# A hybrid layer on one core: three sets of RWKV scores, the inverse inside the neighbour's chain, and output-projection pools laid out anew

## The chip, the cores and the metric

The kernel runs on one core of a Trainium2 chip. The metric is device time in microseconds (us) of one launch; the median of three runs is 2404.65 us (2397.96 to 2404.76).

## The reference, cut to what matters

```python
xn = rms_norm(h, norm1_gain); proj = xn @ w_in            # 2048 x 1024 @ 1024 x 3840
ret = silu(gate) * head_norm(retention(q, k, v))          # 4 heads of 128, chunks of 64
rw = rwkv7_time_mix(...)                                  # 8 heads of 64, a strict recurrence
...
def step(state, inp):                                     # RWKV-7, per token
    sa = einsum('bhvk,bhk->bhv', state, a_t)
    state = state * w_t + sa * b_t + v_t * k_t
    return state, einsum('bhvk,bhk->bhv', state, r_t)
...
h = h + concatenate([ret, rw]) @ w_out
h = h + hier_moe(rms_norm(h, norm2_gain), ...)            # best of 4 groups, best 2 of its 8 experts
return rms_norm(h, final_norm_gain)
```

All 2048 tokens are one sequence; data are float32.

## The kernel before, in words

The program is written as a stream of operations with priorities; a scheduler that knows each tile's readers and writers turns the stream into one fixed queue for each engine (PE for matmuls, DVE, ACT and POOL for elementwise work, SP for issuing transfers). An engine runs its queue strictly in order, so an instruction that waits holds back all that stands behind it. A tile is a buffer out of a pool: a pool of n buffers lets n tiles live at once, the next waits until the oldest has no readers left. Pools are opened from the left or the right end of the on-chip memory, and what is opened later on the same end may lie over a pool that was closed, and then waits for its last users.

**Phase A, about 0 to 1260 us.** Four groups g of 512 tokens. `norm_b` scales eight slices of x into `nT`; `rwkv_proj` and `ret_head` project them with W_in. Each float32 product is three matmuls over a high and a low part of both factors (`split_w` makes the parts on ACT and DVE). Retention then runs `core(g, h)` for four heads, each a chain of matmuls in the PSUM pool `pk` of one bank with evictions between them; the very last head, (3, 3), takes the pool `pj` of two banks instead. The projection matmuls `pj<-nT,whl` are long and independent, and fill PE wherever something else waits.

RWKV runs in 16 units u of 128 tokens, in steps:

- `rwkv_prep(u)`: loads features, forms decays, makes the score tiles `ar` and `pt` (matmuls `pb<-ar,bk`), and `bkt`, `uv`, `bon`, `wc` for the chain;
- the solve (labelled solve{u} in the stream, inside `rwkv_prep`): pieces of `pt` go to DRAM (`nl_d`) and come back as `ln`, POOL runs 62 small instructions `tm`, `xl` one after the other, and SP stores `xl_d` and loads it back as `t1s`, `t2s` and `inv`;
- `rwkv_inv(u)`: a transpose of `t1s` on PE, called the turn here (`psi<-cst,t1s`), and eight small matmuls with evictions complete the inverse;
- `rwkv_chain(u)`: two halves c that carry the state `sbd`: `psr`, times the inverse into `psz`, `uv`, `pss_`, output `yt`;
- `rwkv_fin(u)`: head norm of `yt`, gate, and the store `mx_d<-yt`.

In the group loop the calls stand in the order prep(u), inv(u), fin(u-2), chain(u-1), and the last fin and chain follow behind the loop.

**Phase B, about 1260 to 1560 us.** `tile2(t)` is W_out on 16 token tiles: eight k-slices of the mixed rows `mx_d` come back, are split into `mT`, and 48 matmuls `acc<-wo,mT` fill two PSUM banks of the pool `accr` (three banks). DVE adds the residual rows (`w<-in_x_dram` for tiles 0 to 7 from the pool `hxp` of three buffers, `raw<-in_x_dram` for 8 to 15 from the pool `rwp` of eight). `post(tiles)`, for one or two tiles, stores h, transposes it with the constant `ct`, computes router logits with `wrt`, runs some 45 small DVE operations for the top choices, scales the rows with `g2b` into `xt_d`, and sums the choices (`os`) on PE for the slot numbers. The constants ct, g2b, wrt, brt, g2c lie in the pool `k2`, the small router tiles in `s2`, both on the right end.

**Phase C, 1560 us to the end.** The experts: weights arrive by DMA, PE is busy without a break. Nothing in it moves but names of buffers.

Of the kernel before, what the change touches and what calls it, by code (L numbers as in the profile page):

```python
# [34 lines left out]
NFS = 6  # L35
FB = (2, 2, 2, 2, 2, 2, 2, 1, 1)
# [96 lines left out]
def build(tc, A, out, dbg=None, phases=3):  # L133
# [17 lines left out]
    def mm(o, l, r, start=True, stop=True):  # L151
        PE.matmul(o, l, r, start=start, stop=stop)  # L152
# [31 lines left out]
    gc, xp, ntp = gp("gc", 1), gp("xp", 1), gp("ntp", 1)  # L184
    wh, wr, ev, rk, rc = gp("wh", 3), gp("wr", 4), gp("ev", 3), gp("rk", 2), gp("rc", 4)
    pj, pkb = gp("pj", 2, space=PSUM), gp("pk", 1, space=PSUM)
    if True:
# [93 lines left out]

        def norm_a(g):
# [14 lines left out]
            xs = []  # L297
            for k in range(8):
                xs.append(xp.tile([128, 512], F32, name=f"x{k}"))
                SY.dma_start(xs[k], A["xt"][k * 128:(k + 1) * 128, g * G:(g + 1) * G])  # L300
# [5 lines left out]
        def norm_b(g):  # L306
# [7 lines left out]
            for k in range(8):  # L314
                n = ntp.tile([128, 2, 512], F32R, name=f"nT{k}")
                with soon():
                    (GP if k in XPL else V).tensor_tensor(xs[k], xs[k], rsb, op=ALU.mult)
                    SC.activation(n[:, 0], xs[k], AF.Copy, scale=g1c[:, k:k + 1])
                    V.scalar_tensor_tensor(n[:, 1], xs[k], g1c[:, k:k + 1], n[:, 0].bitcast(F32),  # L319
                                           op0=ALU.mult, op1=ALU.subtract)  # L320
                nT.append(n)
            return nT

        def lora(g, fo):
# [7 lines left out]
            def job(j, f):  # L332
# [5 lines left out]
                t = xp.tile([128, 512], F32, name=f"x{j * 4 + f}")  # L338
# [44 lines left out]
        def rwkv_prep(u):  # L383
            t0 = u * 128
            mk(f'prep{u}')
            ar = rp.tile([128, 4, 2, 128], F32, name="ar", bufs=2)
            pt = rp.tile([128, 4, 2, 2, 128], F32, name="pt", bufs=2)
            bkt = rp.tile([128, 2, 512], F32, name="bkt", bufs=2)
            uv = rp.tile([128, 2, 512], F32, name="uv", bufs=2)
            bon = rp.tile([128, 4, 128], F32, name="bon", bufs=3)  # L390
            wc = rp.tile([128, 4, 2], F32, name="wc", bufs=2)
# [5 lines left out]
            c8 = lambda x: x.rearrange("p (c t) -> p c t", t=64)  # L397
            lg = tr.tile([128, 128], F32, name="lg", bufs=3)
            kt, sg_, ta, rt, vt = tmp(), tmp(), tmp(), tmp(), tmp()
# [42 lines left out]
            psb = pb.tile([128, 4, 128], F32, name="pb")  # L442
            mm(psb.rearrange("p f t -> p (f t)"), blk2, rt)
            V.tensor_tensor(bon, psb, f3(vt), op=ALU.mult)
            psv = pb.tile([128, 512], F32, name="pb")
            for i in range(4):
                PE.transpose(psv[:, i * 128:(i + 1) * 128], f3(vt)[:, i], ident)
            uvh = uv.rearrange("p c (f h v) -> p c f h v", h=2, v=64)
            GP.memset(uvh[0:64, :, :, 0], 0.0)
            GP.memset(uvh[64:128, :, :, 1], 0.0)  # L450
            for c in range(2):
                pv = psv[c * 64:c * 64 + 64].rearrange("p (f h v) -> p f h v", h=2, v=64)
                SC.copy(uvh[64:128, c, :, 0], pv[:, :, 0])
                SC.copy(uvh[0:64, c, :, 1], pv[:, :, 1])
            for i in range(0, 4, 2):
# [10 lines left out]
                pst = pb.tile([128, 2, 2, 128], F32, name="pb")  # L466
                for q in range(4):
                    PE.transpose(pst[:, q % 2, q // 2], bk[:, i * 2 + q], ident)
                SC.copy(bkt[:, :, i * 128:(i + 2) * 128], pst.rearrange("p c f x -> p c (f x)"))
# [19 lines left out]
            for q in range(4):  # L489
                SY.dma_start(xl_d[u].rearrange("l (r q) t -> q l r t", q=4)[q], xl[q * 32:(q + 1) * 32])  # L490
            ST[u] = (ar, pt, bkt, uv, bon, wc, lg)

        def rwkv_inv(u):
# [17 lines left out]
            PE.transpose(ps[:, 0].rearrange("p f x -> p (f x)"), t1s.rearrange("p f x -> p (f x)"), ident)  # L511
# [12 lines left out]
        def rwkv_chain(u):  # L524
            ar, pt, bkt, uv, bon, wc, lg = ST.pop(u)
            tt = inv_[u % 2]
            mk(f'chain{u}')
            for c in range(2):
# [19 lines left out]
                for f in range(4):  # L548
                    mm(pss_[:, f], bkt[:, c, f * 128:(f + 1) * 128], uv[:, c, f * 128:(f + 1) * 128], f == 0, f == 3)
# [105 lines left out]
        for g in range(NG):  # L655
# [7 lines left out]
            for u in range(u0, u0 + 4):  # L663
                with tc.high_priority(offset=PRW):
                    rwkv_prep(u)
                with tc.high_priority(offset=PRC):
                    rwkv_inv(u)
                if u >= 2:
                    with tc.high_priority(offset=PRF):
                        rwkv_fin(u - 2)  # L670
                if u >= 1:
                    with tc.high_priority(offset=PRC):
                        rwkv_chain(u - 1)
            if g == NG - 1:
                with tc.high_priority(offset=PRC):
                    rwkv_fin(4 * NG - 2)
                    rwkv_chain(4 * NG - 1)
                    rwkv_fin(4 * NG - 1)
# [14 lines left out]
    rwp, tpp, accl = lp("rwp", NRAW), lp("tpp", 2, space=PSUM), lp("accl", 3, space=PSUM)  # L693
# [647 lines left out]
```

## Time and profile before

| what | value |
|---|---|
| median of 3 runs | 2404.65 us |
| the profiled execution's own time | 2402.56 us |
| its span on the core | 2400.8 us |
| mean granted TensorE clock | 0.954 of full speed |
| PE busy, DVE busy, ACT busy | 2196.5, 1698.5, 1157.2 us |
| first matmul of the output projection | 1260.2 us |
| first matmul of the experts' phase | 1560.1 us |

The profiled execution is 2.1 us under the median. PE is the engine to watch: what matters is where it stands idle and what ended that idle time, and the clock at which it ran.

### The profile page before, as it was taken

How to read it: one execution, taken by the hardware profiler on the slowest of the kernel's cores; microseconds unless marked ns; L12 is line 12 of the kernel's file. 1: busy time of each engine (PE TensorE's matmuls, PEld its weight loads, DVE VectorE, ACT ScalarE, POOL GpSimd, SP SyncE). 2: the span in 40 equal slices, each digit the busy share in tenths (PEclk: the TensorE clock that was granted, in tenths of full speed). 3: DMA queues.
4: the chain of work that ended last, by engine and by line, in shares of the span. 5: the costliest groups of instructions: out<-in, count | busy, mean ns of one | idle time of the engine just before them, and what ended most of it. 6: DMA issues, size and time to landing. Idle time of an engine off the chain costs nothing. (4 is left out here: it accounts for less than half of the span.)

```text
span 2400.8 us, 36373 instructions
## 1 busy us (share of the span) xinstructions
PE 2196.5 (91%) x11816; PEld 1803.3 (75%) x11817; DVE 1698.5 (71%) x3594; ACT 1157.2 (48%) x1963; POOL 779.1 (32%) x1405
## 2 busy tenths in 40 slices
PE   5999889998998989999879999599999999999990
PEld 4887678887777877788768888577777777777770
DVE  4477775878766787667775665767777777777775
ACT  4353443434434344343332232267777677776763
POOL 2036444354531575146541433411112111111110
PEclk9999899999999999999969999799999999999995
DMA  6643254433544325433234445289999999999978
GB/s 212 211 148 99 82 172 135 135 94 99 173 142 122 98 88 167 125 101 99 84 96 130 127 163 175 94 304 306 307 321 299 304 300 320 310 293 303 310 233 297
DMA packets 291298, 454.78 MB, mean 189 GB/s; under 512 B 93392, under 2 KB 164496, under 8 KB 291088
## 3 DMA queue, kind: packets, MB, share of 16 engines
q1 hardware_dynamic: 277136, 414.10, 51.7%
q0 software_dynamic: 13824, 37.80, 7.0%
q8 instruction: 94, 1.54, 0.3%
q14 instruction: 100, 0.82, 0.1%
q10 hardware_dynamic: 144, 0.52, 0.1%
HBM read 375.18 MB, written 81.85 MB: 190 GB/s over the span
## 5 line engine op out<-in xcount | busy, mean ns | idle before, releaser
L152 PE MATMUL pj<-nT,whl 128*128 128x512 f32 x2496 | 628.1, 403 | 9.2 <-DVE nT L319 5.2
L152 PEld LDWEIGHTS pj<-nT,whl 128*128 128x128 f32 x2496 | 466.3, 192 | 107.0 <-DVE nT L319 5.7
L914 DVE TENSOR_TENSOR hl<-raw,hl 128x1024 fp32r<-128x1024 f32 x384 | 448.5, 1219 | 121.5 <-ACT hl L913 121.5
L152 PE MATMUL acc<-hl,xT 128*128 128x512 f32 (+1 forms) x2048 | 508.1, 400 | 0.0
L152 PEld LDWEIGHTS acc<-hl,xT 128*128 128x128 f32 (+1 forms) x2048 | 365.0, 182 | 100.0 <-ACT xT L172 0.2
L913 ACT CAST hl<-raw 128x1024 fp32r<-128x1024 f32 x384 | 378.4, 1048 | 6.7 <-PE tp L152 3.0
L249 ACT CAST whl<-wraw 128x512 fp32r<-128x512 f32 x248 | 152.5, 618 | 299.3 <-PE pj L152 236.1
L250 DVE TENSOR_TENSOR whl<-wraw,whl 128x512 fp32r<-128x512 f32 x248 | 188.0, 761 | 144.2 <-ACT whl L249 138.1
L152 PE MATMUL acc<-hl,hT 128*128 128x512 f32 (+1 forms) x1024 | 249.5, 398 | 0.0
L152 PEld LDWEIGHTS acc<-hl,hT 128*128 128x128 f32 (+1 forms) x1024 | 183.1, 181 | 51.8
L486 POOL TENSOR_TENSOR tm<-xl,ln 128x60 f32<-128x60 f32 (+24 forms) x496 | 173.8, 350 | 105.2 <-DMA ln<-nl_d 60.4
L488 POOL TENSOR_TENSOR xl<-xl,tm 128x60 f32<-128x60 f32 (+24 forms) x496 | 195.3, 394 | 36.6
L152 PE MATMUL acc<-wo,mT 128*128 128x512 f32 x768 | 192.3, 402 | 0.0
L1147 POOL DMA_INDIRECT h_d<-yo,ti x48 | 80.1, 1670 | 299.3 <-ACT yo L1139 180.1
L1014 POOL DMA_INDIRECT xb<-xt_d,ti x48 | 49.5, 1031 | 369.6 <-PE tp L1025 288.0
L152 PEld LDWEIGHTS acc<-wo,mT 128*128 128x128 f32 x768 | 142.3, 191 | 28.7 <-DVE mT L169 0.2
L152 PE MATMUL pj<-whl,nT 128*128 128x256 f32 x768 | 114.3, 298 | 0.3 <-DVE gs L600 0.2
L464 DVE TENSOR_TENSOR pt<-pb,cst 64x512 f32<-64x512 f32 x128 | 88.0, 687 | 22.6 <-PE pb L152 20.8
L152 PEld LDWEIGHTS pj<-whl,nT 128*128 128x128 f32 x768 | 101.6, 199 | 3.0 <-DVE gs L600 0.5
L499 POOL COPY mbd<-pt 32x128 f32<-32x128 f32 x64 | 20.7, 323 | 222.9 <-DVE pt L464 199.1
L172 ACT CAST xT<-tp 128x512 fp32r<-128x512 f32 x80 | 47.0, 588 | 82.6 <-PE tp L1025 54.4
L152 PE MATMUL pb<-ar,bk 64*128 64x128 f32 x512 | 76.3, 295 | 5.2 <-DVE pt L464 3.7
(445 smaller groups left out, 3184.5 us busy)
## 6 DMA issues: line engine op xcount, KB each, us to landing
raw<-in_wg_dram SPq DMA_DIRECT2D x128, 512.0 KB
raw<-in_wu_dram SPq DMA_DIRECT2D x128, 512.0 KB
raw<-in_wd_dram SPq DMA_DIRECT2D x128, 512.0 KB
wraw<-in_win_dram SPq DMA_DIRECT2D x208, 256.0 KB
tr<-pf_d SPq DMA_DIRECT2D x80, 256.0 KB
pf_d<-ev SPq DMA_DIRECT2D x52, 256.0 KB
x<-in_xt_dram SPq DMA_DIRECT2D x32, 256.0 KB
pf_d<-x SPq DMA_DIRECT2D x32, 256.0 KB
```

The costliest lines, as they stand in the source:

```text
L152: PE.matmul(o, l, r, start=start, stop=stop)
L172: SC.copy(dst_h, ps)
L249: SC.copy(hl[:, 0], raw)
L250: V.tensor_tensor(hl[:, 1], raw, hl[:, 0].bitcast(F32), op=ALU.subtract)
L464: V.tensor_tensor(pt[zs, i:i + 2, :, z ^ h], psp[h][zs].rearrange("p (f c) x -> p f c x", f=2), maskp[zs, None, None, :].to_broadcast([64, ...
L486: GP.tensor_tensor(tv, xl[:, 0:r, t:t + 1].to_broadcast([128, r, n]), ln[:, t:t + 1, t + 1:32].to_broadcast([128, r, n]), op=ALU.mult)
L488: GP.tensor_tensor(xl[:, 0:r, t + 1:32], xl[:, 0:r, t + 1:32], tv, op=ALU.add)
L499: GP.tensor_copy(mbd[i * 32:(i + 1) * 32, :, i * 32:(i + 1) * 32], pt[i % 2 * 64:i % 2 * 64 + 32, :, i // 2, 0, 32:64])
L913: (SC.copy if hi is SC else hi.tensor_copy)(hl[:, 0], raw)
L914: lo.tensor_tensor(hl[:, 1], raw, hl[:, 0].bitcast(F32), op=ALU.subtract)
L1014: return GP.indirect_dma_start(out=xbs[b], out_offset=None, in_=xt_d, in_offset=bass.IndirectOffsetOnAxis(ap=ti[b][:, e:e + 1], axis=0), b ...
L1147: GP.indirect_dma_start(out=h_d, out_offset=bass.IndirectOffsetOnAxis(ap=idx, axis=0), in_=y, in_offset=None, bounds_check=S + 127, comput ...
```

## The change

Instruction counts by engine are the same before and after; only order, waits and memory places differ. There are four parts.

1. The tiles `ar`, `pt`, `wc` get three buffers instead of two, and in `rwkv_prep` the part that makes `bon`, `uv`, `bkt` stands behind the solve instead of ahead of it.
2. `rwkv_inv(u + 1)` is called inside `rwkv_chain(u)`, behind the `pss_` matmuls of the first half, and a dependency that costs no semaphore keeps the turn behind them. The loop runs prep(u), chain(u-2), fin(u-3).
3. The ring of x slices has four tiles instead of eight, `wr` three instead of four buffers, and head (3, 3) of retention uses `pk` like the others.
4. The pool `accr` becomes `accs` (one bank) and `accr` (two), taken in turn; each weight tile `wo` has a pool of its own; loading pools `mrp` and `mxp` are larger and apart; splits of the weights and of the first three tiles have the chain's priority; `k2`, `s2` and `rwp` lie on the left end now, over RWKV's pools.

```diff
-            ar = rp.tile([128, 4, 2, 128], F32, name="ar", bufs=2)
-            pt = rp.tile([128, 4, 2, 2, 128], F32, name="pt", bufs=2)
+            ar = rp.tile([128, 4, 2, 128], F32, name="ar", bufs=3)
+            pt = rp.tile([128, 4, 2, 2, 128], F32, name="pt", bufs=3)
...
-        def rwkv_inv(u):
+        def rwkv_inv(u, behind):
...
-            PE.transpose(ps[:, 0].rearrange("p f x -> p (f x)"), t1s.rearrange("p f x -> p (f x)"), ident)
+            turned = PE.transpose(ps[:, 0].rearrange("p f x -> p (f x)"), t1s.rearrange("p f x -> p (f x)"), ident)
+            if behind:
+                tc.add_manual_dep(turned.ins, behind.ins.name, mybir.DependencyInfo(
+                    mybir.DependencyClass.NoSync, mybir.DependencyReason.DATA))
...
-                    mm(pss_[:, f], bkt[:, c, f * 128:(f + 1) * 128], uv[:, c, f * 128:(f + 1) * 128], f == 0, f == 3)
+                    last = mm(pss_[:, f], bkt[:, c, f * 128:(f + 1) * 128], uv[:, c, f * 128:(f + 1) * 128], f == 0, f == 3)
+                if c == 0 and u + 1 < 4 * NG:
+                    rwkv_inv(u + 1, last)
...
-            pk = pj if (g, h) == (NG - 1, 3) else pkb
-            pkn = "pj" if pk is pj else "pk"
+            pk, pkn = pkb, "pk"
...
+            for u in range(u0, u0 + (4 if g < NG - 1 else 7)):
+                if u < 4 * NG:
+                    with tc.high_priority(offset=PRW):
+                        rwkv_prep(u)
...
+                if u >= 2 and u - 2 < 4 * NG:
+                    with tc.high_priority(offset=PRC):
+                        rwkv_chain(u - 2)
+                if u >= 3:
                     with tc.high_priority(offset=PRF):
-                        rwkv_fin(u - 2)
...
+                        rwkv_fin(u - 3)
...
-    rwp, tpp, accl = lp("rwp", NRAW), lp("tpp", 2, space=PSUM), lp("accl", 3, space=PSUM)
-    k2, s2, accr = kp("k2", 1), kp("s2", 2), kp("accr", 3, space=PSUM)
-    mrp, wop7, wop, hxp, xhp, mtp = gp("mrp", 2), gp("wop7", 1), gp("wop", 1), gp("hxp", 3), gp("xhp", 2), gp("mtp", 2)
+    k2, s2, rwp = lp("k2", 1), lp("s2", 2), lp("rwp", NRAW)
+    tpp, accl, accs, accr = lp("tpp", 2, space=PSUM), lp("accl", 3, space=PSUM), kp("accs", 1, space=PSUM), kp("accr", 2, space=PSUM)
+    mrp, mxp, mtp = gp("mrp", 4), gp("mxp", 2), gp("mtp", 2)
+    wop = [gp(f"wop{k}", 1) for k in range(7, -1, -1)][::-1]
+    hxp, xhp = gp("hxp", 3), gp("xhp", 2)
```

Place 1 is SP's queue where the constants of phase B are loaded. Before, they stand behind the first stores of unit 14's scores (`nl_d`) and ahead of nearly all of RWKV's last two units; two more units' `mx_d<-yt` stores come later.

```order
L474 DMA nl_d<-pt 32x8x32 x2
L737 DMA mraw<-mx_d 128x4x128
L481 DMA ln<-nl_d 32x1024 x4
L652 DMA mx_d<-rc 128x512
L737 DMA mraw<-mx_d 128x4x128
L698 DMA ct<-in_cst_dram 128x476
L703 DMA g2b<-in_g_dram 128x1024
L705 DMA wrt<-in_wr_dram 128x288
L707 DMA brt<-in_br_dram 128x36
L712 DMA g2c<-in_g2c_dram 128x8
L400 DMA lg<-pf_d 128x128
L580 DMA mx_d<-yt 128x4x128
```

After, they stand directly behind the last store of unit 15, `mx_d<-yt`, and the eight residual tiles and the first stores of `xt_d` stand behind them.

```order
L591 DMA mx_d<-yt 128x4x128 x2
L707 DMA ct<-in_cst_dram 128x476
L712 DMA g2b<-in_g_dram 128x1024
L714 DMA wrt<-in_wr_dram 128x288
L716 DMA brt<-in_br_dram 128x36
L721 DMA g2c<-in_g2c_dram 128x8
L760 DMA raw<-in_x_dram 128x1024 x8
L880 DMA xt_d<-w_13081 128x1024
L880 DMA xt_d<-w_13145 128x1024
L760 DMA w_13273<-in_x_dram 128x1024
L760 DMA w_13491<-in_x_dram 128x1024
```

So the load of `ct` moved from before unit 15's solve to the end of unit 15, with the same neighbours behind it on the queue.

Place 2 is PE's queue at the end of unit 15. Before, the last transposes of fin15 (`psi<-cst,yt`) and its gate product (`psi<-lg,lw`) stand among the matmuls of the output projection.

```order
L152 MATMUL acc<-wo_12977,mT 128x512 x6
L152 MATMUL acc<-wo_12976,mT 128x512 x6
L152 MATMUL acc<-wo_12975,mT 128x512 x6
L572 MATMUL psi<-cst,yt 128x128 x4
L152 MATMUL acc<-wo_12982,mT 128x512 x3
L152 MATMUL acc<-wo_12981,mT 128x512 x2
L152 MATMUL tp<-os,ct 128x32 x5
L152 MATMUL acc<-wo_12981,mT 128x512
L152 MATMUL acc<-wo_12980,mT 128x512 x3
L152 MATMUL acc<-wo_12979,mT 128x512 x3
L152 MATMUL acc<-wo_12978,mT 128x512
L152 MATMUL psi<-lg,lw 128x128 x4
```

After, the last chain matmuls, both steps of fin15 and the whole first post (`tp<-ct`, `tp<-wrt`, `tp<-os`) stand in one row, and the next matmuls of the output projection (tile 4's) behind them.

```order
L153 MATMUL psz<-uv,bkt 128x128 x4
L153 MATMUL psr<-uv,pt 64x64 x4
L153 MATMUL psz<-uv,pt 64x64 x4
L583 MATMUL psi<-cst,yt 128x128 x4
L153 MATMUL psi<-lg,lw 128x128 x4
L785 MATMUL tp<-ct,w_13081 128x128 x8
L153 MATMUL tp<-wrt,xh 128x36 x8
L785 MATMUL tp<-ct,w_13145 128x128 x8
L153 MATMUL tp<-wrt,xh 128x36 x8
L153 MATMUL tp<-os,ct 128x32 x5
L785 MATMUL tp<-ct,w_13209 128x128 x4
L153 MATMUL acc<-wo_13006,mT 128x512 x3
```

What moved is the filler: between the chain's last matmul and the sum of choices of post 0 there is no matmul of the output projection left.

Place 3 is PE's queue at a turn in the second group (that of unit 4 in both; line 511 before, 517 after). Before, the turn follows projection matmuls, and score matmuls of the next unit come right behind it.

```order
L152 MATMUL pj<-nT_3263,whl 128x512 x3
L152 MATMUL pj<-whl,nT_3235 128x256 x3
L152 MATMUL pj<-whl,nT_3239 128x256 x3
L152 MATMUL pj<-whl,nT_3235 128x256 x3
L511 MATMUL psi<-cst,t1s 128x128
L152 MATMUL pb<-ar,bk 128x128 x4
L619 MATMUL pk<-cst,kT 128x128 x4
```

After, it stands among projection matmuls in the same way, and next come those of the decays.

```order
L153 MATMUL pj<-nT_3099,whl 128x512 x3
L153 MATMUL pj<-nT_3105,whl 128x512 x3
L153 MATMUL pj<-nT_3069,whl 128x512 x2
L517 MATMUL psi<-cst,t1s 128x128
L153 MATMUL pj<-nT_3069,whl 128x512
L153 MATMUL pj<-nT_3073,whl 128x512 x2
L153 MATMUL pb<-tr,cst 128x512
```

What moved are the scores of the next unit: they no longer follow the turn directly, and projection matmuls stand on both sides of it.

## Rows read from the trace of the kernel before

**Rows 1.** The page: busy time by engine, then the granted TensorE clock by slices.

```profile
PE 2196.5 (91%) x11816; PEld 1803.3 (75%) x11817; DVE 1698.5 (71%) x3594; ACT 1157.2 (48%) x1963; POOL 779.1 (32%) x1405
...
PEclk9999899999999999999969999799999999999995
```

**Rows 2.** Windows: busy us by engine, clock, DMA share, GB/s.

```profile
1200.00:1250.00 50.00, 34.39 (x201) 30.80 (x199) 39.72 (x107) 19.92 (x43) 20.26 (x48) 0.67 0.39 108
1400.00:1450.00 50.00, 50.00 (x301) 43.81 (x301) 33.37 (x146) 14.26 (x32) 13.57 (x14) 1.00 0.60 206
1435.00:1440.00 5.00, 5.00 (x28) 4.22 (x27) 4.26 (x21) 2.37 (x6) 0.81 (x2) 1.00 1.03 412
1500.00:1550.00 50.00, 33.49 (x181) 28.51 (x179) 38.33 (x205) 17.57 (x35) 24.25 (x24) 0.82 0.30 101
```

**Rows 3.** Waits of PE up to 1560 us: total, times, longest.

```profile
PE psi L511 <- DMA t1s<-xl_d: 36.0, 15, 3.9
PE pj L152 <- DVE rs_y L164: 16.3, 1, 16.3
```

**Rows 4.** Timeline of unit 4, PE, POOL and SP: scores, solve, turn.

```profile
457.41 0.71 PE L152 MATMUL pb<-ar,bk 64*128 64x128 f32 x4
...
467.06 0.24 POOL L486 TENSOR_TENSOR tm<-xl,ln 128x31 f32<-128x31 f32 x1 [5.77 <-DMA ln<-nl_d]
...
502.84 2.52 SPq L490 DMA_DIRECT2D xl_d<-xl  x4
...
510.19 0.30 PE L511 MATMUL psi<-cst,t1s 128*128 128x128 f32 x1 [2.17 <-DMA t1s<-xl_d]
```

**Rows 5.** Timeline of PE from the last projection matmuls to the output projection.

```profile
1182.64 1.53 PE L152 MATMUL pj<-nT,whl 128*128 128x512 f32 x6
1184.71 0.66 PE L619 MATMUL pk<-cst,kT 128*128 128x128 f32 x4
...
1225.26 1.11 PE L649 MATMUL pk<-cst,rc 128*128 128x128 f32 x4
1228.34 2.08 PE L152 MATMUL pj<-vtm,rc 128*128 128x128 f32 x8 [1.11 <-ACT rc L621]
...
1249.14 1.11 PE L152 MATMUL psr<-uv,pt 64*64 64x64 f32 x8 [6.28 <-ACT yt L540]
...
1260.17 3.61 PE L152 MATMUL acc<-wo,mT 128*128 128x512 f32 x10
```

**Rows 6.** Timeline of unit 15's last steps: PE, DVE, POOL.

```profile
1403.04 0.42 DVE L561 TENSOR_TENSOR yt<-yt,psz 64x256 f32<-64x256 f32 x1
...
1412.27 1.05 POOL L379 TENSOR_TENSOR yt<-yt,rs_y 128x512 f32<-128x512 f32 x1 [6.61 <-DVE rs_t L162]
...
1418.81 1.13 DVE L575 SCALAR_TENSOR_TENSOR yt<-psi,pcol,bon 128x128 f32<-128x128 f32 x4 [2.93 <-PE psi L572]
...
1422.63 1.06 PE L152 MATMUL psi<-lg,lw 128*128 128x128 f32 x8
...
1423.73 0.69 DVE L579 TENSOR_TENSOR yt<-yt,psi 128x512 f32<-128x512 f32 x1 [1.48 <-issue]
```

**Rows 7.** Timeline of SP and DVE: constants, residual rows, stores.

```profile
1316.48 0.33 SPq L862 DMA_DIRECT2D xt_d<-w  x1
1319.96 0.34 SPq L742 DMA_DIRECT2D w<-in_x_dram  x1
...
1327.47 0.69 DVE L754 TENSOR_TENSOR w<-acc,w 128x512 f32<-128x512 f32 x1 [2.02 <-PE acc L152]
...
1424.49 0.36 SPq L580 DMA_DIRECT2D mx_d<-yt  x1
1424.90 4.20 SPq L742 DMA_DIRECT2D raw<-in_x_dram  x5
```

**Rows 8.** Timeline of PE at the end of the output projection.

```profile
1527.44 1.33 PE L767 MATMUL acc<-ct,raw 128*128 128x128 f32 x8
...
1540.23 1.04 PE L152 MATMUL tp<-os,ct 128*128 128x32 f32 x4 [5.04 <-DVE oh L822]
```

More of the change, by code (lines that the diff above doesn't have):

```diff
@@ L35 @@
 NFS = 6
+NXB = 4
 FB = (2, 2, 2, 2, 2, 2, 2, 1, 1)
@@ L151, in mm @@
     def mm(o, l, r, start=True, stop=True):
-        PE.matmul(o, l, r, start=start, stop=stop)
+        return PE.matmul(o, l, r, start=start, stop=stop)
     def rsqrt(pool, v, n, tag):
@@ L280, in build, with xcols @@
         XN = {}
+        def xcols(g, k):
+            x = xp.tile([128, 512], F32, name=f"x{k % NXB}")
+            SY.dma_start(x, A["xt"][k * 128:(k + 1) * 128, g * G:(g + 1) * G])
+            return x
         def norm_a(g):
@@ L296, in norm_a @@
                     SC.activation(xt, xt, AF.Square, accum_out=ss[:, tt, hf:hf + 1])
[L297 to L300, printed above, removed]
+            xs = [xcols(g, k) for k in range(NXB)]
             v = sm.tile([128, 4], F32, name="v1")
@@ L385, in rwkv_prep @@
             mk(f'prep{u}')
[L386 to L391 removed]
+            ar = rp.tile([128, 4, 2, 128], F32, name="ar", bufs=3)
+            pt = rp.tile([128, 4, 2, 2, 128], F32, name="pt", bufs=3)
+            wc = rp.tile([128, 4, 2], F32, name="wc", bufs=3)
             def tmp(tag="tr", **kw):
@@ L524, in rwkv_chain @@
         def rwkv_chain(u):
-            ar, pt, bkt, uv, bon, wc, lg = ST.pop(u)
+            ar, pt, bkt, uv, bon, wc, lg = ST[u]
             tt = inv_[u % 2]
@@ L720, in build @@
         SY.dma_start(h_d[S:S + 128, :], A["x"][0:128, :])
-        wo = [(wop7 if k == 7 else wop).tile([128, 2, 1024], F32R, name=f"wo{k}") for k in range(8)]
+        wo = [wop[k].tile([128, 2, 1024], F32R, name=f"wo{k}") for k in range(8)]
         for k in range(7, -1, -1):
@@ L726, in build, with acct @@
                 SY.dma_start(raw, A["wout"][k][:, hs])
-                split_w(wo[k][:, :, hs], raw)
+                with tc.high_priority(offset=PRC):
+                    split_w(wo[k][:, :, hs], raw)
+        NA = [0]
+        def acct():
+            NA[0] += 1
+            return (accs if NA[0] % 3 == 0 else accr).tile([128, 512], F32, name="acc")
         def w4(t):
@@ L742, in tile2 @@
             SY.dma_start(hx, A["x"][r0:r0 + 128, :])
-            ps = [accr.tile([128, 512], F32, name="acc") for _ in range(2)]
+            ps = [acct() for _ in range(2)]
             for k in range(7, -1, -1):
@@ L1197, in build @@
                 nps = 2 if w == 2 else 1
-                PS[(2 * e, w)] = [accr.tile([128, 512], F32, name="acc") for _ in range(nps)]
+                PS[(2 * e, w)] = [acct() for _ in range(nps)]
                 if more(e):
```

74 lines of the change are left out of this document (35 added, 39 removed).

## The prediction

> **What bounds the kernel now.** I read the page first. PE is busy for 91% of the span, and the clock row is full except at the start, around 1200 us and around 1500 us [rows 1]. So phase C, where nothing moves, can't change the time, and neither can most of the output projection: between 1400 and 1450 us PE is busy for all 50 us at full clock [rows 2]. What can change is idle time ahead of 1560 us. The list of PE's waits up to there names the largest group: the turn of the inverse, which stood 15 times for the transfer `t1s<-xl_d`, 36.0 us in all, 3.9 at most. The next, 16.3 us once, is the start of the kernel, where the first norm has no cover [rows 3]. Two stretches have more loss than any single row: 1200 to 1250 us, where PE is busy for 34.39 of 50 us at a clock of 0.67, which is a mixture of the two levels, and 1500 to 1550 us, 33.49 us at 0.82 [rows 2]. The first of these is the end of RWKV and retention, the second the last routers; the second has no edit in it.
>
> The reader should see two things about the turn's wait. It ends on a transfer, not on a buffer: for unit 4 the last score matmul ends at 458.1, POOL's solve starts at 467.06, its result is stored at 502.84 and the turn starts at 510.19, 52 us after the scores [rows 4]. And it is short because some 45 us of PE work stand in between. A third set of scores shortens none of these steps; only the amount of PE work in between can change the wait.
>
> **The start.** Four x tiles instead of eight hold up the second four loads until the first four are used. In the new order the early splits go ahead of these loads. From the spacing of these rows I take a gain of 2.5 us, bounds 0 and 3 (the wait there is 16.3 us [rows 3], and most of it is the norm itself).
>
> **The turns.** By the order, with every matmul at the mean pitch of its kind in the trace, PE work between a unit's last scores and its turn was 46.4 us in the mean of the first 14 units and is 48.5 us now. The same distance in time was 50.8 us in the mean, in which PE stood idle for 5.5 us, 2.4 of them at the turn. If each unit took this mean, 2.1 us for each of 14 turns would go, 30 us. But solves differ: over 16 units they took 25 to 45 us, since POOL's other work is put between their 62 instructions. Exchanging for every unit the POOL work that stands inside its solve, and taking the larger of what its solve then asks for and what was idle for other reasons, I get 74 us of idle time in these windows in place of 77. I take a gain of 5 us, with bounds of a gain of 30 and a loss of 8. Moving `uv`, `bkt` and `bon` behind the solve moves matmuls that fill PE, not a step of the path; I cost it at nothing, and its cover is the same projection.
>
> At this place a rule of the Trainium skill speaks for a larger gain. Perfetto Trace Analysis, section Optimization Strategy, says that a gap which repeats on the engine that should be saturated can mean that there isn't enough SBUF or PSUM for the next tile. By this rule a third set would take away the whole group. The rows show a releaser that is a transfer, so I give the rule only the chance of the rival below.
>
> **The end of RWKV.** The last projection matmul ended at 1184.2 and the output projection began at 1260.17, 76 us later [rows 5]. By the order these hold about 40 us of PE work, so some 36 us were lost, waits such as 6.28 us at 1249.14 and half clock together. Head 2 held the bank `pk` from 1184.71 to 1226.4, 41.7 us, while the first part of head 3 ran in `pj` beside it; its second part began at 1228.34 [rows 5]. After the change both heads take `pk`, one after the other, about 80 us at the same price each. On the other side the units are ahead by about one, so that the last chains fall into the same stretch, and 36 matmuls of the first output tile fill in: 68 us of PE work where 40 were. Two heads of 40 us, with what follows up to unit 14's second half, make some 97 to 101 us, that is 29 to 33 us lost in place of 36. I take a gain of 4 us, with bounds of a gain of 11 and, if a head takes 48 us, a loss of 10.
>
> **The end of unit 15: a new stall.** This is the decisive term. The chain's last eviction began at 1403.04, and the last step of fin15 ended at 1424.42 [rows 6]. That cost nothing, since matmuls of the output projection stood in PE's queue all the way [rows 2]. In the new order none do. The queue goes from the chain's last matmul through both steps of fin15 to the whole of post 0. And post 0 can't begin: `ct` lies over RWKV's tiles, and its load stands on SP behind `mx_d<-yt` of unit 15, which waits for fin15's last multiplication. Why isn't PE given W_out tiles there? Their three residual buffers are taken by tiles 0 to 2, which only the posts free; tiles 3 and 4 have filled the three banks by then. The price, step by step:
>
> - From the chain's end to POOL's scaling: 1403.04 to 1413.32, 10.3 us, with other DVE work of some 2 us between; 9 us, bounds 8.2 and 10.3 [rows 6].
> - Transposes, gain rows (1.13 us), gate product (1.06) and last multiplication (0.69), handovers included: 4 us, bounds 3.5 and 6.3 (the latter with other matmuls between) [rows 6].
> - SP's issue of the store: 0.4 us [rows 7].
> - From the issue of `ct` to the next matmul of the output projection: two paths, the longer counts. One is the router. The shortest that the trace has, for a single tile with PE idle, takes 12.8 us from the transposes at 1527.44 to the sum of choices at 1540.23 [rows 8]; with two tiles some 14, and 3 ahead of it for the landing of `ct` (a store and the load that waits for it stand 3.5 us apart [rows 7]): 17 us. The other is the residual row of tile 3. Its load waits for a store of post 0, and ahead of that store stand `ct`, `g2b` and eight tiles of 0.52 MB, 5.1 MB in all, 12.5 us at the 412 GB/s that loads of this kind reached [rows 2]; then 3.5 us for the store, 3.5 for the load, and twice 0.69 us for the eviction [rows 7]: 21 us. I take 20, bounds 16 and 24.
> - Less 8 us of PE's own work in this row (32 small transposes and matmuls of the posts and fin15).
>
> The sum is 9 + 4 + 0.4 + 20 - 8 = 25.4 us, bounds 20 and 33. Two more us for the half clock that such a gap brings (after 5.0 and other idle us the stretch from 1500 has 0.82 [rows 2, 8]), bounds 0 and 6, and 2 us for tiles 5 to 7, whose buffers come in the same way, bounds 0 and 5: about 30 us, and from 20 to 44. The routers are late with it, but their end and all of phase C move by the same amount; nothing there can give it back, since PE was already full [rows 2].
>
> A second rule of the Trainium skill bears on this. DMA: Bandwidth & Descriptors, section Queues, rings and completion order, says that on each engine descriptors are consumed in ring order. By it the store and the load of tile 3 come behind all 5.1 MB, as in the second path; without it the router's 17 us would count, and the stall would be 3 us shorter.
>
> **The sum.** The profiled execution took 2402.56 us, 2.1 under the median of the runs shown. 2402.6 - 2.5 - 5 - 4 + 30 = 2421 us.
>
> **The rivals.**
>
> - *The turns' waits go, and it gets faster.* For it: the larger PE work in each of the 14 windows, worth 30 us if solves are regular. Against it: the spread of the solves. With the stall at its lower bound of 20, the end of RWKV at 8 and the start at 2.5: 2402.6 + 20 - 30 - 8 - 2.5 = 2382. It decides where turns and RWKV's end together give back more than the stall takes, some 28 us. Chance 0.18.
> - *The parts cancel; the change does nothing that can be measured.* The stall at 20 and the turns at 12: 2402.6 + 20 - 12 - 4 - 2.5 = 2404. Chance 0.17.
> - *One bank for both heads costs more.* If the last heads take 48 us each, and the stall comes to 36: 2402.6 + 36 + 10 - 5 - 2.5 = 2441. For it: the heads wait on evictions that now compete with units running ahead. Against it: head 3 had to wait for `pk`'s evictions on the same engines before. Chance 0.15.
> - My forecast, its own range 2411 to 2433: chance 0.50.
>
> A difference under 0.3%, 7.2 us, is about what can't be told from no change. The first rival is faster (0.18), the second the same (0.17), the other two slower (0.65). The range, 2388 to 2444, reaches into the first rival and takes in the third.
>
> **What would show it.** PE's waits should have a new group: the first transposes `tp<-ct,w`, ended by the load of `ct`, 10 us or more after fin15, and the first matmul of tile 4 behind it, ended by DVE; in some 35 us around them PE is busy for 8 to 12. The turns should still wait, 25 to 35 us in all. From the last projection matmul to the end of the last head it should take 85 to 95 us. The prediction is wrong if the turns' waits fall below 10 us in all, if tile 4 starts within 15 us of the chain's end, or if new waits on score buffers or on loads of x appear ahead of 1100 us.

## The result and the profile after

The changed kernel is slower: 2440.87 us in the median of four runs (2434.74 to 2442.3), against 2401.31 us for the kernel before (2394.65 to 2404.76); the ratio is 1.0163, with an interval of 1.0132 to 1.0195. That is 39 us by the ratio. The forecast was slower by 18, with a range that just holds the result. The profiled execution took 2434.74 us, 32 more than that of before, so some 6 us of the loss stand in no trace.

The page of the profile after, to be read against [rows 1]: PE's busy time grows by 15.5 us with the same number of matmuls, and the clock row has more slices below 9.

```profile
PE 2212.0 (91%) x11816; PEld 1821.7 (75%) x11817; DVE 1698.2 (70%) x3594; ACT 1159.7 (48%) x1963; POOL 765.6 (31%) x1405
...
PEclk9999899989899998999969699889999999999995
```

Windows of after (columns as in [rows 2]). The stretch from 1400 us is full as before. The one from 1350 us is new: PE is busy for 28 us of 50, at a clock of 0.62, which is a mixture of the two levels (1.2 and 2.4 GHz).

```profile
1200.00:1250.00 50.00, 38.76 (x247) 34.47 (x247) 39.89 (x104) 19.18 (x40) 28.89 (x69) 0.78 0.36 102
...
1350.00:1400.00 50.00, 28.04 (x139) 24.63 (x138) 24.31 (x102) 11.44 (x28) 7.09 (x7) 0.62 0.47 164
1400.00:1450.00 50.00, 50.00 (x274) 42.81 (x273) 22.73 (x84) 14.11 (x31) 11.78 (x12) 1.00 0.50 156
```

That stretch on PE, in order of time, is the stall that was forecast. From the chain's last matmul (`psz<-uv,pt`, which ends at 1354.0) to tile 4's first (`acc<-wo` at 1392.46) no matmul of the output projection runs, and each bracket is a wait with nothing to fill it.

```profile
1353.38 0.65 PE L153 MATMUL psz<-uv,pt 64*64 64x64 f32 x8 [0.45 <-DVE sbd L563]
1362.13 1.12 PE L583 MATMUL psi<-cst,yt 128*128 128x128 f32 x4 [8.10 <-POOL yt L384]
1364.54 2.08 PE L153 MATMUL psi<-lg,lw 128*128 128x128 f32 x8 [1.29 <-DVE yt L586]
1370.80 1.97 PE L785 MATMUL tp<-ct,w 128*128 128x128 f32 x8 [4.18 <-DMA ct<-in_cst_dram]
1374.52 3.60 PE L153 MATMUL tp<-wrt,xh 128*128 128x36 f32 x16 [1.75 <-DVE rs_t L164]
...
1379.75 1.12 PE L785 MATMUL tp<-ct,w 128*128 128x128 f32 x4 [0.73 <-ACT xh L787]
...
1389.58 2.32 PE L153 MATMUL tp<-os,ct 128*128 128x32 f32 x10 [5.46 <-DVE os L843]
...
1392.46 5.52 PE L153 MATMUL acc<-wo,mT 128*128 128x512 f32 x18
```

SP's queue shows why `ct` is late: its load is issued 0.4 us behind unit 15's last store, with nothing between. The last line, from DVE, adds up tile 3 with its residual row.

```profile
1367.43 0.36 SPq L591 DMA_DIRECT2D mx_d<-yt  x1
1367.83 0.51 SPq L707 DMA_DIRECT2D ct<-in_cst_dram  x1
...
1370.55 4.47 SPq L760 DMA_DIRECT2D raw<-in_x_dram  x8
...
1389.51 1.29 DVE L772 TENSOR_TENSOR w<-acc,w 128x512 f32<-128x512 f32 x2
```

PE's waits up to 1600 us, against [rows 3]: the turn is still there, now with three releasers (below, and one of 3.4 us on `inv<-xl_d`), 40 us in 12 turns in place of 36 in 15.

```profile
PE psi L517 <- DMA t1s<-xl_d: 29.4, 10, 6.7
PE psi L583 <- POOL yt L384: 22.8, 5, 8.1
PE pj L153 <- DVE rs_y L165: 16.6, 1, 16.6
...
PE psi L517 <- DVE bk L441: 7.4, 1, 7.4
```

SP has a wait that before has not. The load of an x slice waits until DVE has used the slice whose tile it takes, twelve times in phase A. (The outputs of the lora part lie in the same ring, and loads wait for their stores to `pf_d` as well; that isn't new: 14.9 us in 13 waits before, 9.4 in 9 after.)

```profile
SPq L285 <- DVE nT L324: 20.0, 12, 4.1
```

**Where the time went.** I take the loss up to a point as the time there minus the work of the matmuls that PE's queue holds up to it, each at the mean pitch of its kind at full clock; so it counts idle time and half clock together. For the profiled executions:

| loss, us | before | after |
|---|---|---|
| up to the last projection matmul (1184, 1204) | 88.0 | 96.6 |
| from there to the slot numbers (1552, 1585), without the stall | 54.6 | 48.4 |
| in the stall of unit 15 | 0 | 31.2 |

This is an estimate, from one execution of each kernel, and executions of one kernel differ by 8 to 10 us. Its level hangs on the pitch: with the mean distance from one matmul's start to the next as the pitch, the first row is 157 and 168. The difference is 9 to 11 either way.

A second count, busy time times granted clock summed over the windows of 50 us up to 1200, gives 1058 us of work in before and 1041 in after. It can't compare these two: summed over the whole span it gives 2127 and 2109 for the same matmuls. Between kernels of one order it holds (2107 in e8 below, 2109 in e9).

The stall has the forecast size (30), and so has the second row (4 forecast, 6 here, which includes the routers). The first row is the surprise: a gain of 7.5 was forecast for the start and the turns, and phase A lost some 10.

### The profile page after: what moved, and what is told of

Its sections match the earlier page's. It is cut to its first block, busy times and chain, and to the rows that moved or that the text cites. A ratio compares the mean times of both kernels' runs of the same rounds, so it can differ in the third digit from the quotient of the medians.

```text
span 2433.0 us, 36386 instructions
## 1 busy us (share of the span) xinstructions
PE 2212.0 (91%) x11816; PEld 1821.7 (75%) x11817; DVE 1698.2 (70%) x3594; ACT 1159.7 (48%) x1963; POOL 765.6 (31%) x1405
## 5 line engine op out<-in xcount | busy, mean ns | idle before, releaser
L153 PE MATMUL pj<-nT,whl 128*128 128x512 f32 x2496 | 635.6, 408 | 12.4 <-ACT nT L323 5.8
L153 PEld LDWEIGHTS pj<-nT,whl 128*128 128x128 f32 x2496 | 472.8, 195 | 118.2 <-ACT nT L323 7.1
L251 DVE TENSOR_TENSOR whl<-wraw,whl 128x512 fp32r<-128x512 f32 x248 | 180.1, 729 | 159.6 <-ACT whl L250 155.1
L473 POOL TENSOR_TENSOR xl<-xl,tm 128x60 f32<-128x60 f32 (+24 forms) x496 | 178.9, 361 | 36.7 <-DMA wraw<-in_win_dram 0.2
L603 POOL TENSOR_TENSOR kT<-kT,ev 128x512 f32<-128x512 f32 x16 | 23.7, 1480 | 213.8 <-DVE ev L602 203.5
```

Of the source, the lines that this page charges most:

```text
L153: return PE.matmul(o, l, r, start=start, stop=stop)
L251: V.tensor_tensor(hl[:, 1], raw, hl[:, 0].bitcast(F32), op=ALU.subtract)
L473: GP.tensor_tensor(xl[:, 0:r, t + 1:32], xl[:, 0:r, t + 1:32], tv, op=ALU.add)
L603: GP.tensor_tensor(t1, t1, t_2, op=ALU.add)
```

## The experiments

The first group of runs asks whether the stall can be repaired where it stands. The second and third take the change apart from both ends. Theory A says that the stall at unit 15's end is what makes the change slow and that a local edit shortens it. The theories beside it place the loss elsewhere: in RWKV's phase and the turns, where the stall only takes the place of waits that would stand there anyway (B); in the third set and the new order, with the place of the constants worth nothing (D); or in the memory layout, that is in the constants' end of the memory and in the ring of x (C). All ratios of one group are taken against the same runs of the kernel before.

### First group: the stall, and the ring alone (before: 2400.86)

**e1_ct_early**: the changed kernel, with the pool of the chain's small tiles and that of unit tiles swapped, so that `ct` lies over tiles that come free earlier.

```diff
-    tr, rp, sm, cp = lp("tr", 8), lp("rp", 1), lp("sm", 2), lp("cp", 1)
+    rp, tr, sm, cp = lp("rp", 1), lp("tr", 8), lp("sm", 2), lp("cp", 1)
```

> The changed kernel with RWKV's pool rp opened ahead of tr, so that the constants of phase B lie over score tiles that unit 15's chain gives back, not over tiles of fin15; ct is loaded ahead of the last mx_d store, the order on PE stays. Theory A (the loss is the stall at the end of unit 15, made of an uncovered fin15 and of post 0 that waits for ct and for buffers): the wait for ct (4.2 us) and 2 to 4 us of the router's start go, fin15's own waits (8.1 and 1.3 us) stay: 5 to 8 us faster than the changed kernel, 2433 to 2436 us. Theory B (the loss lies in the RWKV phase, in turns and half clock, and the stall takes the place of waits that would stand there anyway): within 3 us of the changed kernel's 2440.9.

2439.94 us, ratio 1.0153 (1.0136 to 1.0171), within the noise of after. `ct` was issued at 1358.5 in place of 1367.8, and PE no longer waits for it. The stall is 6 us shorter for that, 32.4 us from the chain's end to the next matmul of the output projection (38.4 in after), and at its end stands a new wait, for the residual row:

```profile
1363.38 0.65 PE L153 MATMUL psz<-uv,pt 64*64 64x64 f32 x8 [0.45 <-DVE sbd L563]
...
1390.29 2.31 PE L153 MATMUL tp<-os,ct 128*128 128x32 f32 x10 [6.03 <-DVE os L843]
...
1396.43 3.78 PE L153 MATMUL acc<-wo,mT 128*128 128x512 f32 x8 [2.92 <-DVE w L772]
```

But the chain itself ended 10 us later than in after, so post 0's sum of choices came no earlier (1389.6 in after). The traces are of executions that took 2442.42 us here and 2434.74 in after, and they don't tell whether the edit made these 10 us.

**e2_four_rows**: a fourth residual buffer for the first tiles; the loading pool `mrp` goes back to two, which makes the room.

```diff
-    mrp, mxp, mtp = gp("mrp", 4), gp("mxp", 2), gp("mtp", 2)
+    mrp, mxp, mtp = gp("mrp", 2), gp("mxp", 2), gp("mtp", 2)
-    hxp, xhp = gp("hxp", 3), gp("xhp", 2)
+    hxp, xhp = gp("hxp", 4), gp("xhp", 2)
```

> The changed kernel with four residual buffers instead of three, paid for by two buffers of mrp. Tile 3 of the output projection can then be added up without a post, and in PE's order one more tile stands between the last chain matmul and fin15. Theory A: 10 to 14 us faster than the changed kernel (one tile is 48 matmuls of 0.24 us), 2427 to 2431 us, the wait of fin15's transposes falls from 8.1 to under 2 us. Theory B: within 3 us of the changed kernel.

2444.12 us, ratio 1.0176 (1.0155 to 1.0197). The edit did what it was to do: more W_out matmuls filled the wait ahead of fin15's transposes (8.10 us in after, 0.65 here), and the last matmul of the output projection ended 11 us earlier (1549.1 against 1560.5). Nothing of it arrived. The end of phase B on PE, e2 first and after second:

```profile
1541.06 8.02 PE L153 MATMUL acc<-wo,mT 128*128 128x512 f32 x34
...
1558.69 1.03 PE L153 MATMUL tp<-os,ct 128*128 128x32 f32 x4 [6.55 <-DVE wgt L872]
...
1590.61 0.26 PE L153 MATMUL tp<-perm,ct 32*1 32x32 f32 x2 [11.31 <-DVE perm L980]
```

```profile
1555.87 4.60 PE L153 MATMUL acc<-wo,mT 128*128 128x512 f32 x19
...
1573.07 1.04 PE L153 MATMUL tp<-os,ct 128*128 128x32 f32 x4 [5.02 <-DVE os L843]
1585.06 0.26 PE L153 MATMUL tp<-perm,ct 32*1 32x32 f32 x2 [10.96 <-DVE perm L980]
```

The reader should see the new wait of 6.55 on DVE: the routers' chain is what ends phase B. From post 0's first sum of choices to the last one it took 189 us in before, 183 in after, and 187 here (1391.7 to 1578.3). From that first sum to the slot numbers (`tp<-perm`) it is 195 to 211 us in every trace of this document, from e8 (1320.4 to 1527.4) to e5 (1435.8 to 1635.8). Whoever gives PE more filler without starting post 0 earlier only moves the idle time behind the matmuls.

**e3_both**: both edits together.

> The last two edits together. Theory A: the two act on different parts of the stall, 15 to 20 us faster than the changed kernel, 2421 to 2426 us. Theory B: within 4 us of the changed kernel.

2441.8 us, ratio 1.0162 (1.0145 to 1.0180). No more than each alone. Theory A falls in its local form for e2 and e3: the 10 to 14 and 15 to 20 us that it gave them lie outside the intervals. For e1 it gave 5 to 8 us, and that much the intervals of e1 and after (9 us together) don't rule out.

**e4_ring_alone**: the kernel before, with four x tiles and three buffers for `wr`.

```diff
+NXB = 4
-    wh, wr, ev, rk, rc = gp("wh", 3), gp("wr", 4), gp("ev", 3), gp("rk", 2), gp("rc", 4)
+    wh, wr, ev, rk, rc = gp("wh", 3), gp("wr", 3), gp("ev", 3), gp("rk", 2), gp("rc", 4)
...
-                xs.append(xp.tile([128, 512], F32, name=f"x{k}"))
+            x = xp.tile([128, 512], F32, name=f"x{k % NXB}")
```

> The kernel before with the x ring of four tiles and three wraw buffers alone. Prediction's step: 0 to 3 us faster at the start, nothing else: 2398 to 2402 us. Theory B's part (the smaller ring sets off half clock behind the first projection, worth 4 to 5 us in the changed kernel's trace): 2402 to 2406 us, with a clock below 1 between 50 and 100 us.

2432.39 us, ratio 1.0122 (1.0095 to 1.0149). This run alone is no verdict on the ring: with the tiles gone, everything behind them moved in memory, some weight tiles of phase B came to lie over `nT`, and the first matmul of the output projection came at 1307 us (1260 in before).

### Second group: the ring, the constants, and two sets (before: 2400.51)

**e5_constants_left**: the kernel before, with the constants' pools on the left end, and nothing else.

```diff
-    k2, s2, accr = kp("k2", 1), kp("s2", 2), kp("accr", 3, space=PSUM)
+    k2, s2, accr = lp("k2", 1), lp("s2", 2), kp("accr", 3, space=PSUM)
```

> The kernel before with one move alone: the pools k2 and s2 (constants and small router tiles of phase B) opened on the left end, behind rwp. Theory C (the place of these pools on RWKV's end of the memory holds the first post back until the last unit is through, and the routers, one after the other, then set the end of phase B): post 0 begins behind fin15, 30 us slower or more, 2430 to 2470 us. Theory D (the third set and the new order of the units lose the time, and the place of the constants is nothing): 2397 to 2406 us.

2475.01 us, ratio 1.031 (1.0285 to 1.0336): 74 us for one line. `ct` was issued at 1404.6 (1234.6 in before), and the row of steps is the one of after, wait for wait:

```profile
1414.12 1.12 PE L572 MATMUL psi<-cst,yt 128*128 128x128 f32 x4 [8.11 <-POOL yt L379]
...
1435.80 2.31 PE L152 MATMUL tp<-os,ct 128*128 128x32 f32 x10 [5.46 <-DVE os L825]
```

In before, post 0's first sum stood at 1351.2. It is 85 us late here, and the slot numbers come 84 us late (1635.8 in place of 1552.2). So the loss is larger than the stall itself: the start of the routers moves, and with it the end.

**e6_ring_padded**: e4 with four unused x tiles added, which hold the memory places of before.

```diff
+        for z in range(4, 8):
+            xp.tile([128, 512], F32, name=f"x{z}")
```

> The kernel before with the x ring of four tiles and three wraw buffers, and four unused tiles that keep the weights' and nT's places as they were, so that the output projection isn't held back as in the run of the ring alone. Theory C: the smaller ring costs 8 to 12 us along the projections, 2409 to 2413 us, with about 99 us instead of 88 lost up to the last projection matmul. Theory D: within 4 us of the kernel before.

2422.95 us, ratio 1.0104 (1.0077 to 1.0132): 25 us by the ratio and 22 by the medians, now without the disturbance of e4 in the places. So the ring costs far more than its start, and more than the 8 to 12 us of theory C. It does not cost it where theory C said, though. The last projection matmul came only 4 us later than in before (1188.0 against 1183.8), while unit 15's last transposes (`psi<-cst,yt`) came 21 us later (1438.8 against 1418.1), post 0's first sum 12 us (1363.0 against 1351.2) and the slot numbers 18 us (1570.3 against 1552.2). In this order it is RWKV's units and the posts that are late, not the projections.

**e7_two_sets_right**: the changed kernel with two sets, the constants on the right, and the loading pools smaller (`mrp` 2, `mxp` 1). The ring still has four tiles.

```diff
-            ar = rp.tile([128, 4, 2, 128], F32, name="ar", bufs=3)
+            ar = rp.tile([128, 4, 2, 128], F32, name="ar", bufs=2)
...
-    k2, s2, rwp = lp("k2", 1), lp("s2", 2), lp("rwp", NRAW)
-    mrp, mxp, mtp = gp("mrp", 4), gp("mxp", 2), gp("mtp", 2)
+    k2, s2, rwp = kp("k2", 1), kp("s2", 2), lp("rwp", NRAW)
+    mrp, mxp, mtp = gp("mrp", 2), gp("mxp", 1), gp("mtp", 2)
```

> The changed kernel with two sets of scores instead of three, which makes room for k2 and s2 on the right end again (with two mraw buffers and one mx buffer); the inverse stays inside the chain, the ring stays at four. Theory C: post 0 begins ahead of the end of unit 15 and the stall goes, the ring's cost stays: 2405 to 2415 us. Theory D: the waits at the turns go back and the time along the projections with them, 2397 to 2406 us, with 88 us lost up to the last projection matmul.

2407.99 us, ratio 1.0039 (1.0020 to 1.0057).

**e8_two_sets_ring8**: e7 with eight x tiles and four buffers for `wr`, as in before.

```diff
-NXB = 4
+NXB = 8
-    wh, wr, ev, rk, rc, gc = gp("wh", 3), gp("wr", 3), ...
+    wh, wr, ev, rk, rc, gc = gp("wh", 3), gp("wr", 4), ...
```

> The last kernel with the x ring of eight tiles and four wraw buffers again: what is left of the change is the inverse inside the chain, the order of the units, the PSUM pools and the pools of the weights. Theory C: both costs are gone, 2394 to 2404 us, and 8 to 12 us faster than with the ring of four. Theory D: the same as with the ring of four, within 3 us.

2383.04 us, ratio 0.9935 (0.991 to 0.996): faster than before (clear of the noise, though under 1%), and 25 us faster than e7; theory C had put it at 2394 or more. By the first count, the loss up to the last projection matmul is 71.3 us here and 95.0 in e7 (88.0 in before). The end of unit 15 on PE has no stall: `ct` was issued at 921.9, and matmuls of the output projection stand between all steps of the chain, of fin15 and of the posts.

```profile
1319.78 0.67 PE L153 MATMUL psr<-uv,pt 64*64 64x64 f32 x8
1320.38 1.30 PE L153 MATMUL tp<-os,ct 128*128 128x32 f32 x10
...
1321.91 2.56 PE L153 MATMUL acc<-wo,mT 128*128 128x512 f32 x10
...
1341.15 0.67 PE L153 MATMUL psz<-uv,pt 64*64 64x64 f32 x8
...
1342.67 7.54 PE L153 MATMUL acc<-wo,mT 128*128 128x512 f32 x32
```

### Third group: one part at a time on the faster kernel (before: 2396.82)

**e9_ring4_wraw4**: e8 with four x tiles; `wr` keeps four buffers.

```diff
-NXB = 8
+NXB = 4
```

> The kernel of two sets and a ring of eight, with the ring at four and the four wraw buffers kept. If the ring's second four loads are the cost (they hold SP's queue until the first four slices are used): 2402 to 2412 us, like the kernel with ring four and three wraw buffers (2408.0). If the third wraw buffer's loss is the cost: 2380 to 2387 us.

2406.72 us, ratio 1.0041 (1.0026 to 1.0057). e7 and e9 agree, so it is the ring and not `wr`. The loads of x, after first and e8 second: with four tiles 19 semaphore waits stand among the 32 loads and the last load goes out at 897.6 us (18 and 905.8 in e9); with eight there are 2, and it goes out at 646.2.

```profile
L285 SPq DMA_DIRECT2D x<-in_xt_dram x32: 327/328/622, 5.8 to 897.6; - x32
L285 SPq EVENT_SEMAPHORE  x19: 17/17/28, 24.4 to 896.8; - x19
```

```profile
L285 SPq DMA_DIRECT2D x<-in_xt_dram x32: 328/416/1000, 5.8 to 646.2; - x32
L285 SPq EVENT_SEMAPHORE  x2: 17/17/17, 53.2 to 64.8; - x2
```

With eight tiles the next group's loads can run ahead; with four they stand in SP's queue among the stores and loads of RWKV. The largest single wait of PE in e9's phase A behind its start, which e8 does not have, shows such a place from SP by way of POOL and ACT to PE. Loads of x stand around the store of the scores (`nl_d`) and their load (`ln`). POOL begins the solve at 280.32 after 4.44 us of idle time (276.79 in e8). The product `rc<-rc,hs` stands in POOL's queue behind most of the solve, ACT waits 7.49 us for it, and PE 11.16 us for the copy behind that.

```profile
269.82 0.35 SPq L285 DMA_DIRECT2D x<-in_xt_dram  x1
271.57 0.80 SPq L459 DMA_DIRECT2D nl_d<-pt  x2
272.47 1.04 SPq L285 DMA_DIRECT2D x<-in_xt_dram  x2
273.73 1.91 SPq L466 DMA_DIRECT2D ln<-nl_d  x4
...
280.32 0.24 POOL L471 TENSOR_TENSOR tm<-xl,ln 128x31 f32<-128x31 f32 x1 [4.44 <-DMA ln<-nl_d]
...
302.34 1.49 POOL L378 TENSOR_TENSOR rc<-rc,hs 128x512 f32<-128x512 f32 x1
...
303.86 0.60 ACT L379 ACTIVATE pk<-rc 128x512 f32<-128x512 f32 x1 [7.49 <-POOL rc L378]
304.48 0.36 ACT L546 COPY rs__1928<-psr 64x256 f32<-64x256 f32 x1
...
304.90 1.97 PE L153 MATMUL psz<-rs__1928,inv 128*128 128x64 f32 x8 [11.16 <-ACT rs__1928 L546]
```

In e8 the product came at 298.58 and the copy at 302.86, so the delay itself is 1.6 us at the copy. The rest of the 11 us is missing cover: e8 had projection and score matmuls directly ahead of it and no wait there (3.10 us for another releaser shortly before). The ring's cost is spread over phase A; by the second count above (windows of 50 us up to 1200) PE did 1058 us of work in e8 and 1038 in e9, so some 21 of the 25 us are lost by then. The posts are late with it: the first sum of choices stands at 1350.9 in e9 and 1320.4 in e8, the slot numbers at 1557.8 and 1527.4, 30 us apart both times.

**e10_left_new_order**: e8 with the constants on the left.

```diff
-    k2, s2, rwp = kp("k2", 1), kp("s2", 2), lp("rwp", NRAW)
+    k2, s2, rwp = lp("k2", 1), lp("s2", 2), lp("rwp", NRAW)
```

> The kernel of two sets and a ring of eight, with k2 and s2 on the left end as in the changed kernel. Theory C: the whole difference of the changed kernel from the kernel of two sets and a ring of four (33 us) is the place of these pools, so 2410 to 2422 us here, with ct behind the last mx_d store. Rival: a part of it was the third set, which holds units apart; then 2390 to 2408 us.

2411.16 us, ratio 1.0061 (1.0041 to 1.0082), against e8's 0.9935: 30 us. The stall is back with its very waits, `ct` issued at 1337.9:

```profile
1332.16 1.12 PE L583 MATMUL psi<-cst,yt 128*128 128x128 f32 x4 [8.11 <-POOL yt L384]
...
1340.78 1.97 PE L785 MATMUL tp<-ct,w 128*128 128x128 f32 x8 [4.13 <-DMA ct<-in_cst_dram]
...
1360.55 2.31 PE L153 MATMUL tp<-os,ct 128*128 128x32 f32 x10 [5.46 <-DVE os L843]
```

**e11_pools_alone**: the kernel before up to the output projection, with the pools of e8 from there on (`accs` and `accr`, a pool for each weight tile, `mrp` 2 and `mxp` 1, and the priorities of the splits).

```diff
-    rwp, tpp, accl = lp("rwp", NRAW), lp("tpp", 2, space=PSUM), lp("accl", 3, space=PSUM)
-    k2, s2, accr = kp("k2", 1), kp("s2", 2), kp("accr", 3, space=PSUM)
+    k2, s2, rwp = kp("k2", 1), kp("s2", 2), lp("rwp", NRAW)
+    tpp, accl, accs, accr = lp("tpp", 2, space=PSUM), lp("accl", 3, space=PSUM), kp("accs", 1, space=PSUM), kp("accr", 2, space=PSUM)
...
```

> The kernel before in phase A, with the PSUM and weight pools of the kernel of two sets (two accumulator pools, a pool for each weight, mx apart, k2 and s2 on the right). If the gain of 17 us of that kernel comes from these pools: 2382 to 2392 us. If it comes from the inverse inside the chain and the order of the units: 2396 to 2405 us.

2411.66 us, ratio 1.0064 (1.0046 to 1.0081): these pools bring nothing by themselves and cost 15 us in the old order. The gain of e8 is therefore that of the inverse inside the chain and the new order of calls: 0.9935 against 1.0064, 31 us, head (3, 3) on `pk` included.

**e12_head_on_pj**: e8 with the last head back on the pool `pj`.

```diff
-            pk, pkn = pkb, "pk"
+            pk = pj if (g, h) == (NG - 1, 3) else pkb
+            pkn = "pj" if pk is pj else "pk"
```

> The kernel of two sets and a ring of eight, with head (3, 3) on the two banks of pj as before. The prediction's step gave the single bank a gain of 4 us with a loss of 10 as the bound: by it 2387 us; if two heads on one bank cost time, 2373 to 2380 us.

2384.7 us, ratio 0.995 (0.9933 to 0.9967). By the ratios one bank is worth 3.6 us, but the intervals overlap; it fits the forecast of 4 and doesn't prove it. The first matmul of the output projection came at 1253.2 in place of 1182.4 us, a shift of 71 us that hardly changes the end: it is filler that moves.

**The sum.** In us against before, from the ratios times 2401: e8 -16, the ring +25 (e7 against e8), the constants on the left +30 (e10 against e8) give +39, and the changed kernel has +39. So for the third set, with the larger loading pools, nothing is left, within about 12 us (the four intervals together). This takes the two costs as ones that add; no run has two sets with both of them, and none has three sets without them. B and D fall as they stand: with two sets in both, the constants alone cost 30 us (e10), which by B and D should be nothing. What B had right is that a good part of the loss lies in RWKV's phase: the ring's. C holds, with a ring that was taken too small.

## Why the prediction came out as it did

The sign, the decisive mechanism and its size were right. The time was 20 us too low because of one step, the ring of x: it cost 27 us more than forecast, and the new order gave only 7 of them back (16 us by e8, with the pools, where 5 and 4 had been taken for the turns and the end of RWKV).

- **The end of unit 15 (+30 forecast): right.** 31 us by the trace, 30 by e10 against e8. Term by term: the scaling took 8.1 us (9 taken); from there to the issue of `ct` 5.7 us (4.4); from the issue to tile 4 24.6 us (20 taken, bounds 16 and 24). That last one was the router's path, not the residual row's: `tp<-os` waited 5.46 us for DVE, and tile 4's matmul ran directly behind the router's last ones without a wait. For two tiles the router takes 18.8 us from the first transposes to the sum of choices, where 14 was taken from the single tile of [rows 8]; PE's own matmuls ran there at half clock. The residual row's path, 21 us in the prediction, was nearly as long: DVE had added up tile 3 at 1390.8, 23 us behind the issue. So this term came out near 20 although the prediction took the wrong one of the two paths for the longer, and there is some luck in it. The prediction let DMA: Bandwidth & Descriptors of the Trainium skill (section Queues, rings and completion order) stand beside the residual path. No run here shows what that rule costs: the eight rows had landed by 1384.5, and tile 3's load was issued behind that, at 1385.83. Of the signs, the wait for `ct` came, 4 us behind fin15's last matmul and not 10; PE was busy for 17 of the 38 us, not for 8 to 12 of 35, since it ran at half clock; the wait for DVE of the next W_out matmul came in e1 (2.92 us) and e3 only.
- **The start: the step that failed.** "Four x tiles instead of eight hold up the second four loads until the first four are used. [...] I take a gain of 2.5 us, bounds 0 and 3". At the start itself it began so. In after the long run of 70 matmuls began at 23.41 us, and at 27.31 in before, but the lora part then waited for its x tiles (1.90 us at 50.56), and the gain was gone by 100 us. What was missing are the other three groups: there the second four loads wait too, on the one queue that also carries the scores to POOL and back. The step cost 25 us in place of -2.5 in e7 and e9, and 22 to 25 in e6, where it showed up later, at the units' end. The prediction named the sign ("new waits on score buffers or on loads of x appear ahead of 1100 us"), by which it is wrong here, and gave it no price.
- **The turns (-5 forecast): no shorter in this kernel, though the new order itself gains.** The rule of Perfetto Trace Analysis (section Optimization Strategy) in the Trainium skill, that a repeated gap can mean too little room for the next tile, doesn't fit these traces: with a third set the turns still waited 40 us in 12 (25 to 35 forecast), and the sum leaves nothing for the set. In e8, with two sets and a ring of eight, they waited 15.8 us in 8. Against before, the new order with the inverse inside the chain is worth 16 us with the pools, and 31 against the same pools in the old order; the one lies within the bound of 30, the other at it. How much of that is the turns, and how much the move of `uv`, `bkt` and `bon` or the order of the calls, no run separates. In after the ring gave this back: at the last projection matmul the loss, by the first count, is 88.0 in before, 71.3 in e8 and 96.6 in after.
- **The end of RWKV (-4): its length as forecast, its gain not shown.** The last head ended 90 us behind the last projection matmul (85 to 95 forecast). The 3.6 us that e12 gives for the bank are within its noise.
- **The cover that isn't in the chain of waits.** The prediction said that the routers' end moves by the same amount as the stall. e2 shows why: the routers take 183 to 199 us from the first sum of choices to the last in every trace here, whatever PE does in between.

Of the rivals, the first one's mechanism (the order gives back more than 28 us) is real, as e8 shows against e11, but not in this kernel. The third, one bank that costs more, ended at the time that was measured (2441) and for a reason that isn't its own.

Left open: how much of the ring's 25 us is the waiting of SP's queue itself, and how much the changed order that the scheduler makes around the later loads; why the pools of e11 cost 15 us in the old order; and why pools on the left come into use only behind RWKV's last tiles whatever bytes they cover (e1's `ct` went 19 us ahead of the last store, but still behind that of unit 14). The latter is read from the order of the queues, and no run separated it.

## What to carry to other kernels

Before a ring of buffers is halved, look at the queue that refills it and at what else stands on that queue: the price isn't paid at the first use but at every group, and not only by the ring's own readers (25 us here, where the queue's own new waits are 11 to 20 us). When pools change their end of the memory, ask for each constant which last reader its load now stands behind; one line cost 74 us in one order and 30 in the other. Where one chain sets the end of a stage, as the routers do here, ask of each edit whether that chain starts earlier. And a kernel that bundles four parts is best judged by taking away each: the fastest version here keeps the inverse inside the chain and the single pools, with two sets, eight x tiles and the constants on the right, 2383.0 us, ratio 0.9935 (0.991 to 0.996).

## What the runs showed of the hardware

- In this stall the waits cost again as half clock. Between 1354.0 and 1392.5 us PE stood idle for 21.5 us, and the granted clock of 1350 to 1400 is 0.62, a mixture of 1.2 and 2.4 GHz: in windows of 5 us it is 0.50 from 1360 to 1390, and 1.00 again from 1395, behind tile 4's first matmuls. The matmuls in the stretch took some 17 us (38.4 less 21.5) where 7 to 9 would do, so that 8 to 10 of the 31 us of the stall were clock.
- A short load behind a store, both issued one after the other on SP, was in use 3.0 us after its issue, with PE waiting for it (`ct`, 1367.83 to 1370.80).
- The same stall in three kernels (after, e5, e10) has the same waits to 0.01 us at two places: 8.10, 8.11, 8.11 for the scaling, and 5.46 three times for the sum of choices. Waits that agree so closely point to one mechanism.
